# Padded tiles: the start addresses of matmul operands modulo 256 bytes in a two-block transformer kernel

## The chip, the core and the metric

The kernel runs on one core of one Trainium2 chip. The core has five engines with queues of their own: TensorE (PE, with its weight loads listed as PEld), VectorE (DVE), ScalarE (ACT), GpSimd (POOL) and SyncE (SP), and 16 DMA engines that move data between the memory and the on-chip buffer of 128 partitions. A tile lies at one byte address, the same in all its partitions. The metric is the device time of one execution in microseconds (us); the times are medians of some runs.

## What is computed

Two transformer blocks, one after the other, on 256 tokens of width 1024 (batch 1), in float32. Cut to the parts that matter:

```python
def first_block(x, c, ctx, c_ctx, ...):              # two layers
    for layer in range(2):
        ...                                          # adaLN, latent attention over 512 keys, Hyena branch
        x = x + g1 * mix_lat
        x = x + g2 * channel_mixer(rmsnorm(x, norm2_g[layer]) * (1 + sc2) + sh2, layer, ...)
        # layer 0: the context's 256 tokens too, and a dense swiglu of width 2816 on all 512
    return rmsnorm(x, final_g)

def moe_swiglu(h, router, w_gate, w_up, w_down):     # channel mixer of layer 1
    top_val, top_idx = lax.top_k(t @ router, 2)      # 2 of 8 experts for each token
    combine = ...                                    # softmax of the two logits
    for e in range(8):
        out = out + combine[:, e:e + 1] * swiglu(t, w_gate[e], w_up[e], w_down[e])   # width 2816

def second_block(x, c, ...):
    x = sandwich(x, ffn1, ...)     # swiglu, width 2816
    x = sandwich(x, mix, ...)      # chunked attention and a gated linear recurrence
    x = sandwich(x, ffn2, ...)     # swiglu, width 2816
```

## The kernel before

Everything lies transposed, features on the partitions and tokens along the row: 512 columns (256 latent, 256 context) in layer 0, 256 in layer 1's mixer and in the second block. The experts stage works on gathered tokens, up to 128 for each expert.

**Products.** A float32 product is made of three matmuls on operands that are split in a high and a low part (`split`: ACT copies the high part, DVE subtracts it from the source for the low part). `mm3` issues them in the order high·high, high·low, low·high. Each matmul is a weight load of a [128, 128] operand and a stream of 256 or 512 columns of a second one; every matmul of the program has its own load, and the loads of following matmuls overlap the streams (rows PEld and PE).

```python
def mm3(self, out, w, x, start, stop):
    self.mm(out, w[0], x[0], start, False)
    self.mm(out, w[0], x[1], False, False)
    self.mm(out, w[1], x[0], False, stop)
```

**Weights.** A weight tile of 512 KB is loaded into a ring of `raw` tiles (SP's queue), then split into a ring of four pairs `whi` and `wlo`. In the two dense blocks `whi`/`wlo` are the loaded operand and the activations (`h`, `fh`, `mg`, `o`, `rec` in the pools b1 and b3) the streamed one. In the experts stage the roles are the other way: the gathered tokens `xe` (up projections, `acc<-whi,xe`) and the hidden values `hm` (down projection, `y<-whi,hm`) are loaded, and 512 columns of `whi` or `wlo` are streamed (256 in the sixth group of an expert, where the width 2816 leaves a rest). An expert has six groups; each ends its up part with four transposes on PE (`turned`, line 1558), so that a run of equal matmuls is broken there. At the ends of an expert stand `scatter` and, every second one, `gather`.

**Pools.** SBUF is given out in stacks: a pool's tiles lie one behind the other, each rounded up to 32 bytes, and a pool that is opened later starts where the earlier ones end. `cp` and `c1` hold constants; behind them lie `w` (`whi`, `wlo`), `r` (four `raw`), and then either `b1`, `k1` (first block) or `x2` (`xsh`, `xsl`), `r2` (nine more `raw`), `k2` (the experts' tiles, `cmp`, `xe`, `hm0`, `hm1`, `ST`, `ys`), `t2` (`ht`). For the second block `b3` and `k3` are opened behind `x2`, where `r2` to `t2` were. What each tile's size adds moves all that lies behind it.

**Order.** SP and POOL run in the order in which the code stands; PE, DVE and ACT in the order of a scheduler that goes by priorities. Tiles of a ring are reused as their readers finish. The lines that the change touches: `open` (L428, tiles `xsh`, `xsl`), `build` (L651 to L680, constants), `startup` (L725, `tneg`) and `once` inside `moe` (L1643, `cmp`).

Of the kernel before, what the change touches and what calls it, by code (L numbers as in the profile page):

```python
# [8 lines left out]
F32 = mybir.dt.float32  # L9
F32R = mybir.dt.float32r  # L10
# [31 lines left out]
FIRST2 = [("in2", j) for j in range(12, 16)], [(g, 2, i) for i in range(2) for g in "gu"]  # L42
FILTER = 1000
FILTER1 = 3

# [341 lines left out]
class PreNorm:  # L389
# [35 lines left out]
    def open(self):  # L425

        p, sh = self.p, self.parts[0][2]
        hi, lo = (p.xsp.tile([128, 8, 258], F32R, name=n, tag=n, bufs=1) for n in ("xsh", "xsl"))  # L428
        self.xs = [(hi[:, k, :], lo[:, k, :]) for k in range(8)]
        p.split(hi[:, :, 256:], lo[:, :, 256:], sh.unsqueeze(2).to_broadcast([128, 8, 2]))  # L430

# [29 lines left out]
class Prog:  # L461
# [183 lines left out]
    def build(self):  # L645
        nc, tc = self.nc, self.tc
        with ExitStack() as es:
            es.enter_context(tc.manual_schedule(engines={SP, POOL}))
            self.cp = es.enter_context(tc.tile_pool(name="cp", bufs=1))
            self.ps = es.enter_context(tc.tile_pool(name="ps", bufs=1, space=PSUM))  # L650
            self.dp = es.enter_context(tc.tile_pool(name="dp", bufs=1, space=DRAM))  # L651
            cp = self.cp
            self.cv = cp.tile([128, CTOTAL], F32, name="cv")
            self.ident = cp.tile([128, 128], F32, name="ident")
            self.ones = cp.tile([128, 128], F32, name="ones")
            self.epsc = cp.tile([128, 1], F32, name="epsc")
            self.gp = cp.tile([128, 6, 8], F32, name="gp")
            self.sp = cp.tile([128, 8], F32, name="sp")
            self.small = cp.tile([128, 1], F32, name="small")
            self.mod = [cp.tile([128, 2, 48], F32, name=f"mod{l}") for l in range(2)]  # L660
            self.ada = cp.tile([128, 72], F32, name="ada")
            self.gn = cp.tile([128, 16, 8], F32, name="gn")
            self.xt = cp.tile([128, 8, 512], F32, name="xt")
            self.x = [self.xt[:, k, :] for k in range(8)]
            self.xl = [self.xt[:, k, :NT] for k in range(8)]
            self.kspill = [self.dp.tile([128, 2048], F32, name=f"ksp{l}") for l in range(2)]
            self.route = cp.tile([128, 10], F32, name="router")
            self.frn = cp.tile([128, 2, 8], F32, name="frn")

            self.rs = cp.tile([128, 8, 2, 8], F32, name="route")  # L670
            self.cnt = cp.tile([1, 1], I32, name="cnt")
            self.spill = [self.dp.tile([128, 2048], F32, name=f"sp{i}") for i in range(3)]
            nc.vector.memset(self.ones, 1.0)
            nc.vector.memset(self.epsc, EPS)
            self.eps2 = cp.tile([128, 1], F32, name="eps2")
            self.fga = cp.tile([128, 2, 8], F32, name="fga")
            nc.vector.memset(self.eps2, EPS * EPS)
            nc.vector.memset(self.small, 1e-26)
            self.kn, self.early = 512, EARLY[0]
            self.wc, self.turn, self.wbufs, self.wpairs = 1024, [0, 0, 0], [4, 4, 4], []  # L680
            self.hold = ()
            c1 = es.enter_context(tc.tile_pool(name="c1", bufs=1))
            self.rope = c1.tile([128, 2, NT], F32, name="rope")
            self.mcst = c1.tile([128, 128 + 256 + 64 + 64], F32, name="mcst")
            with ExitStack() as s0:
                self.wp, self.rp = (s0.enter_context(tc.tile_pool(name=n, bufs=1)) for n in ("w", "r"))
                with ExitStack() as s1:
                    self.bp = s1.enter_context(tc.tile_pool(name="b1", bufs=13))
                    self.kp = s1.enter_context(tc.tile_pool(name="k1", bufs=1))
                    self.startup()  # L690
                    self.layer0()
                    self.layer1()
                self.xsp = s0.enter_context(tc.tile_pool(name="x2", bufs=1, reuse_waits="tile"))
                self.latter("")

            with tc.If(self.most > 128), ExitStack() as s0:
                self.wp, self.rp, self.xsp = (s0.enter_context(tc.tile_pool(name=n, bufs=1)) for n in ("wg", "rg", "xg"))
                self.latter("g")
# [18 lines left out]
    def startup(self):  # L717
        nc, a = self.nc, self.a
# [3 lines left out]
        hc, hw = (self.b([2048], name=n) for n in ("hc", "hw"))  # L722
        zf = KOFF["zfeat"][0]
        self.dma(hc[:, :256], a["kc"][:, zf:zf + 256])
        self.tneg = self.kp.tile([128, 2], F32, name="tneg")  # L725
        self.dma(self.tneg, a["kc"][:, zf + 256:zf + 258])
        self.dma(hc[:, 512:768], a["hw"][:, :256])
        stages = self.filters(hc, hw)
# [20 lines left out]
        for n, b in enumerate((4, 5, 6, 7, 0, 1, 2, 3)):  # L749
# [20 lines left out]
            for k in range(8):  # L770
                if n not in ADAR:
                    self.mm(acc, cs[:, k, :], w[k // 4][:, k % 4, :], k == 0, k == 7)
                else:
                    hi, lo = w[k // 4][k % 4]
# [4 lines left out]
            for i in range(2):  # L779
                c = 4 * b + 2 * i  # L780
                self.mm(pt[:, c:c + 2], row[:, i * 128:i * 128 + 128], fold[:M], True, True)
            j = 2 * b
            self.tt(m[:, :, j:j + 2], pt[:, 2 * j:2 * j + 4].rearrange("p (b i) -> p i b", i=2),
                    self.col(("bmod", 0), j, 2).unsqueeze(1).to_broadcast([128, 2, 2]), OP.add)
            if n < 4:
                k = j - 8
                self.stt(self.gn[:, 0:2, k:k + 2], m[:, :, j:j + 2], 1.0,
                         self.col(("n1g", 0), k, 2).unsqueeze(1).to_broadcast([128, 2, 2]), OP.add, OP.mult)
                while ready and ready[0] <= k + 1:
                    c = ready.pop(0)  # L790
# [483 lines left out]
    def layer0(self):  # L1274
# [24 lines left out]
        def fill(d):  # L1299
            if d >= FILTER1:  # L1300
                next(filt)
            self.ada_fill(2)
# [114 lines left out]
    def moe(self, tp, general):  # L1417
        nc, kp, tc = self.nc, self.kp, self.tc
# [220 lines left out]
        def once():  # L1639

            for c in range(2):
                self.stt(L[:, c, :], self.lg[c], r[:, c:c + 1], self.route[:, 0:8], OP.mult, OP.add)
            cm = kp.tile([128, 2, 128], F32, name="cmp")  # L1643
            c1, c2 = (cm[:, i, :].rearrange("p (c a b) -> p c a b", c=2, a=8) for i in range(2))
            a = L.unsqueeze(2).to_broadcast([128, 2, 8, 8])
            b = L.unsqueeze(3).to_broadcast([128, 2, 8, 8])
            self.tt(c2, a, b, OP.is_equal)
            self.tt(c2, c2, lt.unsqueeze(1).to_broadcast([128, 2, 8, 8]), OP.mult)
            self.tt(c1, a, b, OP.is_gt)
            self.tt(c1, c1, c2, OP.add)  # L1650
            nc.vector.tensor_reduce(rank, c1, axis=AX.X, op=OP.add)
            masked = self.ts(mask, rank, 1.5, OP.is_lt)
            pp = self.psc(16, "pos")
            self.mm(pp, tri, mask.rearrange("p c e -> p (c e)"), True, False)
            self.mm(pp[:, 8:16], self.ones, mask[:, 0, :], False, True)
            tokens(0, masked)
            nc.vector.tensor_copy(pos, pp.rearrange("p (c e) -> p c e", c=2))

            S0 = onehot(0, 0)
            tokens(1, self.hot)  # L1660
            with tc.issue_after(self.hid):
                self.table(r, AF.Silu)

            pc = self.psc(8, "cnt")
            for c in range(2):
                self.mm(pc, self.ones, mask[:, c, :], c == 0, c == 1)
            nc.vector.reduce_max(rs[:, 7, 1, 0:1], pc, axis=AX.X)
            nc.vector.tensor_copy(self.cnt, rs[0:1, 7, 1, 0:1])
            nc.gpsimd.dma_start(self.spill[0].rearrange("p (a b) -> p a b", a=8), self.xt[:, :, :NT])
            for t, s in zip(ht, self.spill[1:]):  # L1670
                nc.gpsimd.dma_start(s.rearrange("p (a b) -> p a b", a=2), t.bitcast(F32))
            xe = gather(0, S0)
            self.hold = self.got[2:3]
            ready.append(self.whl(*self.last_ahead))
            self.hold = ()
            lows.append(self.lo_ins)
            fetch()
            nxt = {}

            def pair(p):  # L1680
                with tc.issue_after(lows[-8]):
                    nxt["S"] = onehot(0, p)
                nxt["xe"] = gather(p, nxt["S"])
            last = None
            for e in range(NE):
                after = {}
                if e:
                    after[0] = lambda last=last: scatter(*last)
                if e % 2 and e < 7:
                    after[3] = lambda: pair(e // 2 + 1)  # L1690
                elif e % 2 == 0:
                    if e == 0:
                        def late():
                            with tc.issue_after(self.silu), tc.issue_after(lows[-1]):
                                softmax()
                        after[1] = late
                    after[3] = lambda: nxt.update(ST=weights(e // 2, S0))
                y = expert(e, xe, use, used, after)
                last = (e, y, nxt["ST"])
                if e % 2 and e < 7:  # L1700
                    S0, xe = nxt["S"], nxt["xe"]
            return last, lambda: ready
# [276 lines left out]
```

## Time and profile before

| | before |
|---|---|
| median of three runs | 2486.97 us (2485.62 to 2494.7) |
| the profiled execution | 2487.37 us, of which the span is 2484.9 |
| PE busy | 2427.2 us (98%), 13,896 matmuls |
| DVE busy | 1993.1 us (80%) |
| ACT busy | 1499.5 us (60%) |
| POOL busy | 89.2 us (4%) |
| HBM read | 573.87 MB, 233 GB/s over the span |
| experts stage, about | 1045 to 1850 us |
| second block, about | 1850 us to the end |

The profile lists for each instruction when it started and ended. The ends of matmuls are modelled and overlap the next ones, so "mean ns of one" of a matmul is longer than the step from one matmul to the next. How fast PE streams is read from the starts: the timeline gives the start of each group of equal instructions, and the difference of two starts divided by the matmuls between them is the step. Idle time stands with what ended it. The granted clock (PEclk) is a share of full speed.

### The profile page before, as it was taken

The numbers are of one execution on the slowest core, as the hardware profiler recorded it, in microseconds if no ns is written. First come the engines' busy times: TensorE is split into PE (matmuls) and PEld (weight loads), VectorE is DVE, ScalarE is ACT, GpSimd is POOL, SyncE is SP. The second block draws the span as 40 slices with busy tenths as digits, with TensorE's granted clock in tenths as the row PEclk, the third lists the DMA queues.
The fourth block names the chain that finished last, engine by engine and source line by source line (L and its number), as shares of the span: only waits on it lengthen the run. The fifth ranks groups of instructions, "written<-read, shape, count | busy, mean of one in ns | idle before, by whom it ended". The sixth has DMA issues, their size and how long they took to land. (4 is left out here: it accounts for less than half of the span.)

```text
span 2484.9 us, 37467 instructions
## 1 busy us (share of the span) xinstructions
PE 2427.2 (98%) x13896; PEld 2073.1 (83%) x13896; DVE 1993.1 (80%) x3001; ACT 1499.5 (60%) x2214; POOL 89.2 (4%) x170
## 2 busy tenths in 40 slices
PE   8999999999999999999999999999999999999997
PEld 4677887788887898878878888888789999998997
DVE  6787799996878877799888988998986668977555
ACT  6676325422224775687777777777775558667444
POOL 0000010221211000000000000000000000000000
PEclk9999999999999999999999999999999999999999
DMA  7122465787885243799999999999965563444653
GB/s 284 52 87 102 149 223 209 253 290 273 292 290 210 82 142 135 256 364 336 349 341 345 342 345 352 350 333 355 347 232 179 187 212 120 157 168 143 202 182 111
DMA packets 161247, 582.71 MB, mean 235 GB/s; under 512 B 18000, under 2 KB 19536, under 8 KB 159904
## 3 DMA queue, kind: packets, MB, share of 16 engines
q1 hardware_dynamic: 136912, 491.35, 56.0%
q0 software_dynamic: 23600, 88.35, 9.8%
q8 instruction: 111, 1.82, 0.3%
q14 instruction: 80, 0.66, 0.1%
q10 hardware_dynamic: 544, 0.52, 0.1%
HBM read 573.87 MB, written 6.29 MB: 233 GB/s over the span
## 5 line engine op out<-in xcount | busy, mean ns | idle before, releaser
L477 ACT ACTIVATE whi<-raw 128x1024 fp32r<-128x1024 f32 (+1 forms) x902 | 917.9, 1045 | 617.9 <-PE acc L491 385.0
L480 DVE TENSOR_TENSOR wlo<-raw,whi 128x1024 fp32r<-128x1024 f32 (+1 forms) x900 | 1063.6, 1206 | 239.7 <-ACT whi L477 234.0
L491 PE MATMUL acc<-h,whi 128*128 128x256 f32 (+1 forms) x3648 | 840.1, 323 | 9.8 <-ACT h L477 4.6
L491 PEld LDWEIGHTS acc<-h,whi 128*128 128x128 f32 x3648 | 610.0, 189 | 67.8 <-ACT h L477 6.3
L491 PE MATMUL acc<-h,wlo 128*128 128x256 f32 (+1 forms) x1808 | 580.9, 322 | 1.0 <-DVE wlo L480 1.0
L491 PE MATMUL acc<-whi,xe 128*128 128x512 f32 (+1 forms) x1536 | 456.5, 377 | 1.0 <-DVE xe L488 0.7
L491 PEld LDWEIGHTS acc<-h,wlo 128*128 128x128 f32 x1808 | 342.2, 189 | 26.5 <-DVE wlo L480 1.9
L491 PEld LDWEIGHTS acc<-whi,xe 128*128 128x128 f32 x1536 | 280.5, 188 | 54.9 <-DVE xe L488 0.9
L491 PE MATMUL acc<-wlo,xe 128*128 128x512 f32 (+1 forms) x768 | 291.4, 379 | 0.1
L488 DVE SCALAR_TENSOR_TENSOR junk<-wt,rows 128x1024 bf16<-128x1024 f32 x200 | 238.8, 1219 | 4.3 <-DMA wt<-in_w 3.2
L491 PE MATMUL acc<-fh,whi 128*128 128x256 f32 (+1 forms) x1056 | 235.4, 318 | 0.2
L491 PE MATMUL y<-whi,hm 128*128 128x512 f32 x704 | 231.7, 400 | 0.0
L491 PEld LDWEIGHTS acc<-fh,whi 128*128 128x128 f32 x1056 | 174.5, 188 | 14.8 <-DVE fh L480 1.0
L491 PEld LDWEIGHTS acc<-wlo,xe 128*128 128x128 f32 x768 | 144.5, 188 | 30.2 <-DVE wlo L480 3.8
L491 PE MATMUL acc<-fh,wlo 128*128 128x256 f32 (+1 forms) x528 | 167.4, 318 | 0.4 <-DVE wlo L480 0.4
L491 PEld LDWEIGHTS y<-whi,hm 128*128 128x128 f32 x704 | 131.3, 188 | 30.8 <-ACT hm L477 3.1
L491 PE MATMUL y<-wlo,hm 128*128 128x512 f32 x352 | 139.6, 400 | 0.5
L491 PEld LDWEIGHTS acc<-fh,wlo 128*128 128x128 f32 x528 | 99.1, 188 | 7.4 <-DVE wlo L480 0.6
L632 POOL DMA_DIRECT2D wt<-in_w x152 | 81.0, 538 | 344.1 <-DVE junk L488 299.1
L491 PE MATMUL acc<-mg,whi 128*128 128x256 f32 (+1 forms) x384 | 87.7, 321 | 1.0 <-DVE mg L480 1.0
L491 PEld LDWEIGHTS y<-wlo,hm 128*128 128x128 f32 x352 | 66.1, 188 | 18.2 <-DVE wlo L480 3.6
L480 DVE TENSOR_TENSOR a<-a,acc 128x256 f32<-128x256 f32 (+2 forms) x64 | 33.2, 519 | 53.2 <-PE acc L491 52.5
(374 smaller groups left out, 2738.4 us busy)
## 6 DMA issues: line engine op xcount, KB each, us to landing
raw<-in_w SPq DMA_DIRECT2D x890, 512.0 KB, 5.5
wt<-in_w POOLq DMA_DIRECT2D x152, 512.0 KB, 5.9
raw<-in_w SPq DMA_DIRECT2D x24, 384.0 KB, 3.1
xt<-in_x SPq DMA_DIRECT2D x4, 512.0 KB, 9.6
ksp<-hf POOLq DMA_DIRECT2D x2, 1024.0 KB, 6.0
kf<-ksp SPq DMA_DIRECT2D x2, 1024.0 KB, 5.1
sp<-ht POOLq DMA_DIRECT2D x2, 1024.0 KB, 10.7
raw<-in_w SPq DMA_DIRECT2D x8, 256.0 KB, 2.8
```

The source lines that it names most:

```text
L477: return self.nc.scalar.activation(out, in_, func, **kw)
L480: return self.nc.vector.tensor_tensor(out, a, b, op=op)
L488: return self.nc.vector.scalar_tensor_tensor(out, a, s, b, op0=op0, op1=op1, **kw)
L491: return self.nc.tensor.matmul(out, lhsT=lhsT, rhs=rhs, start=start, stop=stop)
L632: self.nc.gpsimd.dma_start(t[:, i, :], self.wsrc(key)[0])
```

## The change

The operations, their order on all five engines and their waits are the same before and after; tiles lie at other addresses.

- Three constant columns of their own (`epsc`, `small`, `eps2`, 32 bytes each with rounding) and `tneg` of the pool `k1` become columns of one tile `few` of 32 bytes. All that lies behind `cp` moves down by 64 bytes, and the tiles of `k1` by 96.
- `cmp`, a tile of the router in `k2`, grows by 40 floats (160 bytes). `S`, `xe`, `hm`, `ST`, `ys` and `ht` lie behind it.
- `xsl` grows by 16 floats (64 bytes). `r2`, and `b3` with `k3` of the second block, lie behind it and so stay where they were.

Where the tiles start, in bytes modulo 256 (worked out by adding the sizes):

| pool, tiles | before | after |
|---|---|---|
| w: `whi`, `wlo` | 64 | 0 |
| r: four `raw` | 64 | 0 |
| b1: all arrays of the first block (`h`, `fh`, `mg`, ...) | 64 | 0 |
| k1: `gq`, `a`, `u`, `ssq`, `nr` | 96 | 0 |
| x2: `xsh`, `xsl` | 64, 128 | 0, 64 |
| r2: nine `raw` | 192 | 192 |
| k2: `xe`, `hm0`, `hm1`, `ST`, `ys` | 96 | 0 |
| k2: `S` | 224 | 128 |
| t2: `ht` | 96 | 0 |
| b3, k3: the second block's arrays and `first` | 192 | 192 |
| cp: `ident`, `ones` | 160 | 160 |
| cp: `xt` | 224 | 192 |

A matmul streams whole chunks of a tile, 128, 256 or 512 columns of 4 bytes apart, so a chunk's residue is that of its tile (but for `xsh` and `xsl`, whose rows have 258 columns).

```diff
+CPAD = 40
+XPAD = 16
...
-        hi, lo = (p.xsp.tile([128, 8, 258], F32R, name=n, tag=n, bufs=1) for n in ("xsh", "xsl"))
+        hi, lo = (p.xsp.tile([128, 2064 + k], F32R, name=n, tag=n, bufs=1)[:, :2064].rearrange("p (a b) -> p a b", a=8)
+                  for n, k in (("xsh", 0), ("xsl", XPAD)))
...
-            self.epsc = cp.tile([128, 1], F32, name="epsc")
+            few = cp.tile([128, 8], F32, name="few")
+            self.epsc, self.eps2, self.small, self.tneg = (few[:, i:j] for i, j in ((0, 1), (1, 2), (2, 3), (3, 5)))
...
-            self.small = cp.tile([128, 1], F32, name="small")
...
-            self.eps2 = cp.tile([128, 1], F32, name="eps2")
...
-        self.tneg = self.kp.tile([128, 2], F32, name="tneg")
...
-            cm = kp.tile([128, 2, 128], F32, name="cmp")
-            c1, c2 = (cm[:, i, :].rearrange("p (c a b) -> p c a b", c=2, a=8) for i in range(2))
+            cm = kp.tile([128, 256 + CPAD], F32, name="cmp")
+            c1, c2 = (cm[:, 128 * i:128 * i + 128].rearrange("p (c a b) -> p c a b", c=2, a=8) for i in range(2))
```

## Rows read from the trace of the kernel before

**Rows 1.** Busy time by stretch: PE, PEld, DVE, ACT, POOL, then PEclk, DMA share, GB/s.

```profile
1045.00:1850.00 805.00, 801.63 (x3824) 652.98 (x3822) 718.31 (x758) 602.45 (x686) 0.00 (x0) 1.00 0.95 344
1850.00:2485.00 635.00, 609.30 (x4921) 597.05 (x4919) 432.00 (x702) 379.60 (x663) 0.00 (x0) 0.98 0.49 162
1100.00:1150.00 50.00, 50.00 (x251) 41.57 (x251) 45.16 (x44) 39.94 (x44) 0.00 (x0) 1.00 0.97 363
```

**Rows 2.** Waits, 1100 to 1840: waiter, releaser, us in total, times, longest.

```profile
ACT whi L477 <- DMA raw<-in_w: 4.2, 10, 0.7
PEld acc L491 <- DVE wlo L480: 3.8, 11, 0.5
```

**Rows 3.** Timeline of PE, layer 0's feed-forward: start, us, instruction, count.

```profile
600.04 0.39 PE L491 MATMUL acc<-h,wlo 128*128 128x512 f32 x1
...
619.76 0.39 PE L491 MATMUL acc<-h,wlo 128*128 128x512 f32 x1
```

**Rows 4.** Timeline of PE, experts stage, 512 columns.

```profile
1377.98 0.40 PE L491 MATMUL acc<-wlo,xe 128*128 128x512 f32 x1
...
1387.77 0.40 PE L491 MATMUL acc<-wlo,xe 128*128 128x512 f32 x1
```

**Rows 5.** Instructions by form, 1045 to 1850: count, busy us, mean ns.

```profile
L491 PE MATMUL acc<-whi,xe 128*128 128x512 f32 x1280 | 409.5, 396 | 1.0 <-DVE xe L488 0.7 <-ACT whi L477 0.2
L491 PE MATMUL acc<-wlo,xe 128*128 128x512 f32 x640 | 255.4, 399 | 0.1
L491 PE MATMUL y<-whi,hm 128*128 128x512 f32 x704 | 231.7, 400 | 0.0
L491 PE MATMUL y<-wlo,hm 128*128 128x512 f32 x352 | 139.6, 400 | 0.5
L491 PE MATMUL acc<-whi,xe 128*128 128x256 f32 x256 | 47.0, 282 | 0.0
L1558 PE MATMUL tp<-ident,xt 128*128 128x128 f32 x176 | 27.0, 272 | 0.0
```

**Rows 6.** Busy time of PE in stretches of layer 0: us, count, PEclk, DMA share, GB/s.

```profile
500.00:520.00 20.00, 20.00 (x90) 1.00 0.58 203
520.00:540.00 20.00, 20.00 (x90) 1.00 0.95 354
```

**Rows 7.** Timeline of PE behind a broken run in layer 0.

```profile
274.94 0.39 PE L491 MATMUL acc<-oh,wlo 128*128 128x512 f32 x1
276.09 0.39 PE L491 MATMUL acc<-h,whi 128*128 128x512 f32 x1
```

**Rows 8.** Timeline of PE, 256 columns: layer 1, then the experts' sixth group.

```profile
900.05 0.28 PE L491 MATMUL acc<-h,wlo 128*128 128x256 f32 x1
901.49 0.28 PE L491 MATMUL acc<-h,wlo 128*128 128x256 f32 x1
1330.91 0.28 PE L491 MATMUL acc<-wlo,xe 128*128 128x256 f32 x1
1336.24 0.28 PE L491 MATMUL acc<-wlo,xe 128*128 128x256 f32 x1
```

**Rows 9.** Timeline of PE, 256 columns, second block: first and last feed-forward.

```profile
1949.83 0.28 PE L491 MATMUL acc<-h,wlo 128*128 128x256 f32 x1
1969.77 0.28 PE L491 MATMUL acc<-h,wlo 128*128 128x256 f32 x1
2419.80 0.28 PE L491 MATMUL acc<-h,wlo 128*128 128x256 f32 x1
2421.24 0.28 PE L491 MATMUL acc<-h,wlo 128*128 128x256 f32 x1
```

**Rows 10.** PE with tile whi, then with tile wlo, 1850 to 2485: us, count.

```profile
1850.00:2485.00 635.00, 546.41 (x3008) 0.98 0.49 162
1850.00:2485.00 635.00, 423.62 (x1504) 0.98 0.49 162
```

**Rows 11.** Layer 0's attention scores, tile gq: count, min/median/max ns, starts, forms.

```profile
L491 PE MATMUL sc<-kt,gq x96: 278/387/503, 102.1 to 218.5; 96*128 96x512 f32 x48, 96*128 96x256 f32 x48
```

## Prediction

> **What bounds the kernel now.** I read the busy times by stretch first, then the waits of the long stretch, then the starts of matmuls in the timeline. In the experts stage PE is busy 801.6 of 805 us at a granted clock of 1.00 [rows 1], and what waits there waits for PE, or briefly: ScalarE waits for a weight tile's DMA 4.2 us in ten places, and a weight load for the low parts 3.8 us [rows 2]. In the second block PE is busy 609.3 of 635 us [rows 1]. So TensorE's own pace sets the time, and since the operations, their order and their waits stay as they are, the change can work only through that pace: the step from one matmul to the next in an unbroken run.
>
> The reader should divide differences of starts. In layer 0's feed-forward 87 matmuls of 512 columns lie between the two low-part rows of [rows 3]: 19.72 us / 87 = 226.7 ns. In the experts stage 42 matmuls of the same shape lie between those of [rows 4]: 9.79 us / 42 = 233.1 ns. Both have the full clock, both run without a gap. In layer 0 the loaded tile (whi, 64) and the streamed one (h, 64) start at equal residues modulo 256; in the experts stage the loaded one is at 96 (xe, hm) and the streamed one at 64 (whi, wlo). I write a case as streamed minus loaded: 0 in layer 0, 224 (32 short of equal) in the experts. Traffic is not what differs: in layer 0 two neighbouring stretches of 20 us hold 90 matmuls each, one with 203 GB/s of DMA beside it and one with 354 [rows 6].
>
> At 256 columns the picture is another: layer 1 (difference 0) takes 1.44 us / 12 = 120.0 ns, the experts' sixth group (224) 5.33 us / 45 = 118.4 [rows 8], the second block (128) 19.94 us / 168 = 118.7 in its first feed-forward and 1.44 us / 12 = 120.0 near its end [rows 9]. So one difference, 128, shows two paces, and equality isn't the faster case there.
>
> **The change part by part.** After it the experts' pairs lie at difference 0, the first block's stay at 0, and the second block's go from 128 to 192.
>
> Experts, 512 columns: 1280 + 640 + 704 + 352 = 2976 matmuls [rows 5], each from 233.1 to 226.7 ns: 2976 x 6.4 ns = 19.0 us less. I take layer 0's step because it is the row with the same shape and the same difference.
>
> Broken runs: the pace has to be found again after a break. In layer 0 the five matmuls behind one took 276.09 - 274.94 = 1.15 us, 230 ns each [rows 7], 3.3 ns over the settled pace. The transposes break the experts' runs 176 / 4 = 44 times [rows 5], scatters and gathers some 16 more: 60 x 5 x 3.3 ns = 1.0 us of the gain is lost.
>
> Experts, 256 columns: 256 of whi [rows 5], and half as many of wlo since mm3 streams the high part twice: 384. From 118.4 to layer 1's 120.0 ns: 0.6 us more.
>
> Second block: 3008 + 1504 = 4512 matmuls on whi and wlo [rows 10], and no row shows a difference of 192. Bounds: a matmul of 256 columns can hardly step faster than half of 226.7, or 113.3 ns, so at best 4512 x 5.4 = 24.4 us less; at worst it pays the same 6.4 ns that 512 columns pay for a bad offset, 28.9 us more. I take nothing, by the nearest rows: 192 lies between 128 and 224, and these show 118.7 and 118.4. The spread of the rows, 118.4 to 120.0, is 1.3 ns about the value taken, or 5.9 us either way.
>
> Small pieces: layer 0's scores with the tile gq (96 to 0) have 48 matmuls of 512 columns [rows 11], at most 48 x 6.4 ns = 0.3 us less, in an attention stage of short runs where I count nothing; if the new address were as bad as the old one is against the settled pace, as much more. The two runs on xsh and xsl, 192 matmuls of 258 columns, could move by 1.2 us either way by the same 6.4 ns. The merged constants add no instruction and no wait.
>
> What must keep up: a triple of matmuls falls from 0.699 to 0.680 us, and the work that feeds it is hidden now. DVE is busy 718.3 of 805 us and would be so of some 787, 91%; DMA would need 344 x 805 / 787 = 352 GB/s where one stretch of 50 us shows 363 [rows 1]. Both fit, so I cost the cover at nothing; if it gave way, part of the gain would turn into waits of ScalarE for weight tiles, and then of weight loads for the split.
>
> Sum: 2487.4 (the profiled execution's own time, 0.4 above the median) - 19.0 + 1.0 + 0.6 = 2470.0, and 2469.6 against the median of 2487.0: **2470**.
>
> **The rivals.** *Addresses are not the cause.* Rows 3 and 4 also differ in which tile is streamed and in what ACT and DVE do beside. Then nothing moves: 2487. For it: only one difference other than 0 is shown at 512 columns. Against it: the steps in the experts stage are as even as those of layer 0, the 14 triples of [rows 4] at 0.69 to 0.70 us, though the work beside them comes and goes. The Trainium skill speaks for this rival: "SBUF — State Buffer", section "Who interferes with whom", gives TensorE two independent read ports, one for the stream and one for the weight load, and says that it never waits on anyone; by that rule the place of two operands could not matter and the time stays at 2487. The two steps of [rows 3, 4] don't fit it, since shape and clock are the same.
>
> *The second block gains as well.* At 192 its runs might settle at a faster pace than any row shows. Half of the bound, 12 us, gives 2458, all of it 2446. For it: difference 128 already shows that two paces are possible [rows 9]. Against: none of four rows at 256 columns is under 118.4.
>
> *The other side.* At 192 the second block's streams and loads hinder each other as they do at 512 columns in the experts stage. At 6.4 ns more for each of 4512 matmuls it is 28.9 us against a gain of 17.4: 2499. It decides from 17.4 us / 4512 = 3.9 ns on, a step of 122.6 ns. Against it: at 256 columns the difference of 224 costs nothing [rows 8]. A small loss, to 120.0 ns everywhere, gives 2476 and belongs to the forecast's own range.
>
> *The feed gives way.* PE asks for weights 2% faster; if DMA or the split held the stage at half of the gain, the time would be 2478. For it: the ten waits for DMA [rows 2]. Against: the 363 GB/s.
>
> **How the numbers follow.** Forecast, experts at 226.7 and the second block within 1.3 ns of now: 0.67, own range 2464 to 2476. No effect of addresses, 2487: 0.09. Second block gains, 2446 to 2462: 0.13. Slower, 2482 to 2499: 0.05. Feed gives way, about 2478: 0.06. The range of 8 in 10 goes from 2455 to 2482: the forecast, the feed, and half of the second block's gain. What a measurement of this kernel can tell from no change is about 0.5%, 12.4 us, or a time under 2474.5. Of the forecast 0.06 lies above that, with the second block near 120.0: faster 0.61 + 0.13 = 0.74, same 0.06 + 0.09 + 0.06 = 0.21, slower 0.05.
>
> **What would show it.** Right: in the timeline of the changed kernel runs of the experts stage step by 226 to 227 ns (triples of 0.68 us), the stage ends some 17 us earlier, layer 0 keeps 226.7, the waits for DMA stay under 10 us, and the second block keeps steps of 118 to 120. Wrong: experts' triples still at 0.70 us (addresses are not the cause); triples at 0.68 with the stage not shorter, and waits of ScalarE on DMA or of weight loads on the low parts in its place (the feed); or the second block's step outside 117.4 to 120.0, which moves the time by 4.5 us for each ns.

## The result, and the profile after

The changed kernel takes 2459.0 us, the kernel before 2490.8, both medians of four runs; the ratio, 0.9871 with a 95% interval of 0.9849 to 0.9894, leaves out one run of the changed kernel that took 3987.8 us at a granted clock of 0.555, so that its other three, 2456.2 to 2460.6 us, stand for it. It is faster by 1.3%. The prediction had the sign and a range that holds the time, but not the make-up of the gain, as its stages show.

Stages can be cut at three starts in the timeline of PE: the first matmul of layer 0 (at 48.6 us in both), the first matmul on the experts' tokens, and the last one on `y`. Here are the last two, first of before, then of after (start, us, instruction, count).

```profile
1047.68 0.50 PE L491 MATMUL acc<-whi,xe 128*128 128x512 f32 x1 [0.73 <-DVE xe L488]
...
1845.64 0.40 PE L491 MATMUL y<-whi,hm 128*128 128x512 f32 x1
```

```profile
1049.64 0.50 PE L495 MATMUL acc<-whi,xe 128*128 128x512 f32 x1
...
1836.12 0.39 PE L495 MATMUL y<-whi,hm 128*128 128x512 f32 x1
```

With the ends of the spans (2484.9 and 2458.1) that makes:

| us | first block | experts | second block |
|---|---|---|---|
| before | 999.1 | 798.0 | 639.2 |
| after | 1001.1 | 786.5 | 622.0 |
| difference | +2.0 | -11.5 | -17.2 |

The +2.0 comes with the clock. PE's matmuls stand in the same order in both, and after falls 2.4 us behind between 206 and 273 us, where its granted clock went down to 0.5 (1.2 GHz, the lower of the two levels) for 6.8 us from 233 us on; over 226 to 250 us PEclk is 0.86 there and 1.00 in before. Just ahead of the fall, from 226 to 233.1 us, PE was busy 5.67 us in after, and 5.76 in before, where the clock stayed. In the runs below that have the first block's differences as in after this stage takes 1000.1 to 1006.4 us. So the experts brought two thirds of what was forecast for them, and the second block, for which nothing was forecast, brought more than the experts.

The page and the busy times by stretch answer to [rows 1]. The stretches of after are the experts stage, the second block, a run of 69 matmuls in the experts stage and a run of 575 in the second block; columns as there.

```profile
span 2458.1 us, 37467 instructions
...
PE 2400.1 (98%) x13896; PEld 2054.5 (84%) x13896; DVE 1991.8 (81%) x3001; ACT 1500.0 (61%) x2214; POOL 89.6 (4%) x170
```

```profile
1047.00:1840.00 793.00, 789.97 (x3821) 650.82 (x3819) 717.00 (x756) 602.17 (x685) 0.00 (x0) 1.00 0.95 350
1840.00:2458.00 618.00, 591.33 (x4922) 578.60 (x4922) 431.83 (x702) 380.32 (x664) 0.00 (x0) 0.98 0.51 167
1213.59:1229.04 15.45, 15.45 (x69) 12.77 (x68) 14.87 (x16) 12.40 (x14) 0.00 (x0) 1.00 0.91 313
1897.38:1962.44 65.06, 65.06 (x575) 65.06 (x575) 33.25 (x37) 33.36 (x49) 0.00 (x0) 1.00 0.60 195
```

The first row reads like that of before: PE is busy 99.6% of the experts stage at the full clock, DVE's work is the same 717 us in a shorter time, and DMA moves 350 GB/s. A stretch that is cut at the first and the last start of an unbroken run holds one step less than matmuls (a matmul or two that still run at its edge may add to the count). So the third row is 68 steps of 512 columns, 15.45 us / 68 = 227.2 ns, and the fourth 574 steps of 256 columns, 65.06 / 574 = 113.3 ns: the value that the prediction held for the floor.

The waits of after between 1100 and 1840 answer to [rows 2].

```profile
ACT whi L481 <- DMA raw<-in_w: 6.3, 13, 1.8
PEld acc L495 <- DVE wlo L484: 6.1, 23, 0.5
```

Both have grown, from 4.2 and 3.8 us, and are still small.

Layer 0 is as in [rows 3]: between these two rows lie 87 matmuls, 19.72 us, 226.7 ns each.

```profile
600.27 0.39 PE L495 MATMUL acc<-h,wlo 128*128 128x512 f32 x1
...
619.99 0.39 PE L495 MATMUL acc<-h,wlo 128*128 128x512 f32 x1
```

### The profile page after: what moved, and what is told of

The parts are those of the page before. It is cut to its first block, busy times and chain, and to the rows that moved or that the text cites. A ratio compares the mean times of both kernels' runs of the same rounds, so it can differ in the third digit from the quotient of the medians.

```text
span 2458.1 us, 37467 instructions
## 1 busy us (share of the span) xinstructions
PE 2400.1 (98%) x13896; PEld 2054.5 (84%) x13896; DVE 1991.8 (81%) x3001; ACT 1500.0 (61%) x2214; POOL 89.6 (4%) x170
## 5 line engine op out<-in xcount | busy, mean ns | idle before, releaser
L495 PE MATMUL acc<-h,whi 128*128 128x256 f32 (+1 forms) x3648 | 829.4, 321 | 9.6 <-ACT h L481 4.6
L495 PE MATMUL acc<-whi,xe 128*128 128x512 f32 (+1 forms) x1536 | 451.0, 373 | 0.3 <-ACT whi L481 0.3
L495 PE MATMUL acc<-fh,whi 128*128 128x256 f32 (+1 forms) x1056 | 230.3, 315 | 0.7 <-DVE fh L484 0.6
L481 ACT ACTIVATE hm<-tp 128x512 fp32r<-128x512 f32 (+1 forms) x48 | 26.9, 561 | 75.0 <-PE tp L1561 74.9
```

The lines of the kernel that those rows point to most:

```text
L481: return self.nc.scalar.activation(out, in_, func, **kw)
L495: return self.nc.tensor.matmul(out, lhsT=lhsT, rhs=rhs, start=start, stop=stop)
```

## The experiments

The theory after the result: what sets PE's step is the residue of the streamed operand minus that of the loaded one, modulo 256 bytes; 512 columns are fastest at a difference of 0, 256 columns at 192. Each experiment gives one stage another difference by the size of a pad, with the order of the work as it was. Its two knobs are CPAD (it moves the experts' tiles) and XPAD (it moves the second block's arrays). In all kernels with a pad alone PE, DVE, ACT and POOL run the same instructions in the same order as in after. Times with a ratio and its interval are medians of five to seven runs; the other kernels ran once, beside one run of before. Single runs of before lie between 2484.4 and 2495.3 us, so that for a kernel that ran once the stages and steps of its trace count, and not its whole time.

### Each half alone

`cpad_only`, the experts at 0 and the second block at 128 as before:

```diff
-CPAD = 40
-XPAD = 16
+CPAD = 56
+XPAD = 0
```

> XPAD 0 and CPAD 56 in the changed kernel: the first block's and the experts' pairs stay at difference 0 as in the changed kernel, the second block's arrays lie at 128, so its difference is 128 as before the change. Theory (the step is set by where the streamed and the loaded operand start modulo 256, each stage for itself): experts settle at 226.7 ns as in the changed kernel, stage about 11 us shorter than before; the second block's feed-forwards step by 118.7 to 120 ns, its span about 634 us; whole time 10 to 12 us under before, about 2476. Rival (the second block's gain comes from the weights at address 0, or from the merged constants): second block at 113.3 ns, whole time about 2459.

`xpad_only`, the second block at 192 and the experts at 224 as before:

```diff
-CPAD = 40
+CPAD = 48
```

> CPAD 48: only the experts' tiles are moved, to 32 modulo 256, so that the experts have difference 224 as before the change (and a start that isn't a multiple of 64), while the second block keeps 192. Theory: experts at 233 ns again, stage 798 us as before, second block at 113.3 and 117.6 ns, 617 us; whole time about 17 us under before, 2470. Rival (the experts' gain is one of absolute places or of traffic): experts stay at 227 to 229 ns and the time at 2459.

Measured: `cpad_only` 2477.9 us, 0.9961 of before (0.9942 to 0.9980), experts 786.0 and second block 635.4 us; `xpad_only` 2476.1 us, 0.9942 (0.9921 to 0.9962), experts 797.8 and second block 623.3 us. The two gains are separate. By the stages they add up, 12.0 us in the experts of the one and 15.9 us in the second block of the other beside 28.7 in both stages of after; the whole times give 9.7 and 14.4 beside 32.1 us, each with an interval of about 5 us either way. The second block of `xpad_only` is 6 us longer than was expected. The same two runs of matmuls that stand above for after, here the experts' 68 steps in before and in `xpad_only`, then the second block's 574 in `cpad_only`:

```profile
1214.36:1230.22 15.86, 15.86 (x70) 12.78 (x68) 15.09 (x16) 12.40 (x14) 0.00 (x0) 1.00 0.90 309
```

```profile
1218.31:1234.17 15.86, 15.86 (x70) 12.77 (x68) 15.08 (x16) 12.39 (x14) 0.00 (x0) 1.00 0.91 312
```

```profile
1899.47:1967.58 68.11, 68.11 (x576) 68.11 (x575) 33.34 (x37) 33.47 (x49) 0.00 (x0) 1.00 0.56 186
```

15.86 / 68 = 233.2 ns and 68.11 / 574 = 118.7 ns: each stage falls back to its old step, with DMA (312 against 313 GB/s), DVE and ACT beside it as in after.

### The experts at other differences

`exp_d192` gives the experts the difference at which the second block gained, `exp_d128` and `exp_d64` the two between:

```diff
-CPAD = 40
+CPAD = 56      # exp_d192;  72 in exp_d128, 88 in exp_d64
```

> CPAD 56: the experts' loaded tiles go from 0 to 64, so that the streamed operand lies 192 beyond the loaded one, as in the second block; all else as in the changed kernel. Theory (192 is the fastest place for any width, and 64-byte starts are all that 512 columns need besides): 512 columns settle at 220 ns (233.1 less two of the 6.67 ns by which the steps so far differ), the experts stage 10 to 20 us shorter than in the changed kernel, time 2440 to 2450. Rival (512 columns are best at equality): 227 to 233 ns, time 2459 to 2471. Second rival (pace is better but the feed takes over): 220 ns in runs, more waits for DMA and low parts, time about 2459.

> The experts' tiles xe and hm start 128 bytes from the weight tiles modulo 256 instead of at the same residue; the second block stays at a difference of 192. Theory (512-column runs have one fast case, equality, at 226.7 ns, and one slow one, 233 ns, everywhere else): experts' steps of 233, the experts stage about 798 us, the run about 2471. Rival (the step grows with the distance from equality, up to half the period): steps over 234 and a stage over 800. Second rival (128 is as good as 0 for 512 columns, the pattern having a period of 128): steps of 227, stage 786, the run 2459.

> The experts' tiles xe and hm at 192 against the weight tiles at 0, or a difference of 64; the second block stays at 192. Theory (equality alone is fast for 512 columns): steps of 233 ns, a stage of about 798 us, the run about 2471. Rival (a sign: differences on one side of equality, as 192 and 224, are slow and those on the other are not): steps of 227, stage 786, the run 2459. At 256 columns 64 is a new difference: no theory gives a value, 113 to 120 ns.

Measured: `exp_d192` 2475.3 us, 0.9935 (0.9913 to 0.9956), experts 797.4; `exp_d128` 2473.9 beside 2494.0, experts 796.6; `exp_d64` 2467.7 beside 2494.0, experts 788.9. The run of 68 steps in `exp_d192`, then in `exp_d64`:

```profile
1221.39:1237.26 15.87, 15.87 (x69) 12.79 (x68) 15.04 (x16) 12.42 (x14) 0.00 (x0) 1.00 0.90 302
```

```profile
1218.72:1234.29 15.57, 15.57 (x69) 12.77 (x68) 14.99 (x16) 12.40 (x14) 0.00 (x0) 1.00 0.93 316
```

233.4 ns at 192 and 229.0 at 64; at 128 the same run takes 232.5. So 192 isn't good for every width, and equality is the best of five differences for 512 columns. But "one fast case, and one slow one everywhere else" falls too: 64 is a third case, nearer to the fast one.

### The first block at 192

`b1_d192` puts a tile of 192 bytes ahead of the first block's arrays:

```diff
-XPAD = 16
+XPAD = 32
+                self.rp.tile([128, 48], F32, name="bpad", tag="bpad", bufs=1)
```

> A tile of 192 bytes ahead of the first block's pools (and XPAD 32): the first block's arrays lie at 192 and its weights at 0, so layer 0 (512 columns) and layer 1 (256 columns) have difference 192 instead of 0; experts at 0 and second block at 192 as in the changed kernel. Theory (192 is the fastest place for any width): layer 0's feed-forward steps by 220 ns instead of 226.7, layer 1 by 113.3 to 117.6 instead of 120; some 3700 matmuls of 512 columns and 1200 of 256 give 20 to 30 us, time 2430 to 2440. Rival (512 columns are best at equality): layer 0 at 226.7 or 233, layer 1 alone gains 3 to 7 us, time 2450 to 2480.

Measured: 2477.5 us, 0.9954 (0.9936 to 0.9971), so some 20 us over after by the two ratios, and the first block 1015.4 us, 14.3 over that of after. Layer 0's longest unbroken run, 1583 steps of 512 columns, in after and then in `b1_d192`:

```profile
444.30:803.14 358.84, 358.84 (x1584) 297.21 (x1583) 293.32 (x467) 111.43 (x147) 67.52 (x126) 1.00 0.76 276
```

```profile
452.91:822.28 369.37, 369.37 (x1585) 297.60 (x1583) 295.33 (x467) 110.68 (x147) 67.25 (x126) 1.00 0.75 268
```

226.7 against 233.3 ns: layer 0, where the roles are the other way (weight tiles are loaded, activations streamed), has the same two steps as the experts. It is the difference, and not the tile or what runs beside it. Layer 1, with 256 columns, went the other way in the same run, from 119.7 to 116.3 ns in the mean of its steps. The run shows one thing more: both pads together move the experts' loaded tiles by 256 bytes against their weight tiles, and the experts stay at 786.6 us and a mean step of 228.7 ns. So a shift of 256 bytes changes nothing, while one of 128 does, as `exp_d128` shows.

### The second block at other differences

`blk2_d0` and `blk2_d64`; the experts stay at 0:

```diff
-CPAD = 40
-XPAD = 16
+CPAD = 24      # blk2_d0;  8 in blk2_d64
+XPAD = 32      # blk2_d0;  48 in blk2_d64
```

> The second block's arrays at the residue of its weights, a difference of 0 instead of 192; the experts stay at 0. Theory (256 columns are slow at equality, as in layer 1): second-block steps of 119 to 120 ns, that stage 637 to 642 us, the run 2475 to 2480. Rival (the second block gained because of another effect of the move than its difference of 192, such as the arrays' distance to each other): steps of 113 to 118 stay and the run takes about 2460.

> The second block's arrays at a difference of 64 from its weights; experts at 0. Nearest known: 256 columns at 0 and 128 take 119 to 120 ns and at 192 113 to 118. Theory (one fast case, 192, as 512 columns have one at 0): steps of 118 to 120 ns, the second block 635 to 641 us, the run 2474 to 2480. Rival (the two odd multiples of 64 are alike, a period of 128): steps of 113 to 118, the block 622 us, the run 2459.

Measured: `blk2_d0` 2480.1 us beside 2494.0, second block 641.9; `blk2_d64` 2477.2 beside 2493.2, second block 631.0. The run of 574 steps in `blk2_d0`:

```profile
1898.21:1967.08 68.87, 68.87 (x575) 68.87 (x575) 33.38 (x37) 33.51 (x49) 0.00 (x0) 1.00 0.57 184
```

and in `blk2_d64`, with its fellow of the same 574 steps in the second feed-forward:

```profile
1905.87:1973.48 67.61, 67.61 (x576) 67.61 (x576) 33.35 (x37) 33.47 (x49) 0.00 (x0) 1.00 0.58 187
2324.28:2389.33 65.05, 65.05 (x575) 65.05 (x575) 35.06 (x40) 32.30 (x48) 0.00 (x0) 1.00 0.63 194
```

At equality 120.0 ns, as in layer 1; the theory holds. At 64 one run goes at 117.8 ns and the like one at 113.3: there are two paces at one difference, and a run keeps the one that it has got into. Neither expectation for `blk2_d64` is right: the block lies between them. The slower of the two paces is found at 192 as well. `exp_d128` has the second block of after, address for address, and there the first of these runs took:

```profile
1906.57:1974.18 67.61, 67.61 (x576) 67.61 (x575) 33.34 (x37) 33.48 (x49) 0.00 (x0) 1.00 0.59 187
```

117.8 ns where after has 113.3. That makes its second block 626.7 us instead of 622.0, and it happened by itself: nothing was changed there. Over all kernels with 192 the second block took 619.5 to 626.7 us.

### The same differences at other addresses

`all32` moves everything behind the constants by 32 bytes, so that no operand starts at a multiple of 64:

```diff
-            few = cp.tile([128, 8], F32, name="few")
+            few = cp.tile([128, 16], F32, name="few")
```

> Everything behind the small constants moves by 32 bytes, so that no operand of the experts or the second block starts at a multiple of 64, while all differences stay as in the changed kernel. Theory (only the difference of the two addresses counts): experts' steps 227 to 229 ns, second block 113 to 118 ns, the run 2456 to 2463. Rival (what counts is that operands start at a multiple of 64 bytes): the experts' steps go back to 233 and the second block's to 119, and the run to about 2487.

Measured: 2461.8 us beside 2494.0, experts 786.3, second block 621.8. The two runs again:

```profile
1215.05:1230.49 15.44, 15.44 (x70) 12.76 (x68) 14.89 (x16) 12.41 (x14) 0.00 (x0) 1.00 0.90 300
```

```profile
1898.56:1963.62 65.06, 65.06 (x576) 65.06 (x575) 33.25 (x37) 33.36 (x49) 0.00 (x0) 1.00 0.62 195
```

227.1 and 113.3 ns: where both operands move by 32 bytes, the steps stay. Layer 0 kept its 226.7 ns as well when both its operands moved by 64 bytes, from before to after. So the difference counts, and not where the two lie, as far as these two moves show.

### Why the experts gained less than forecast

The pair `nobreak_224` and `nobreak_0` is without the transposes that break the experts' runs:

```diff
-                    tp = self.ptp(n)
-                    for i in range(n // 128):
-                        nc.tensor.transpose(...)
-                    self.split(t[0], t[1], tp)
+                    self.split(*(x.rearrange("p (a b) -> p a b", a=c) for x in t), a)
```

> The experts stage without the transposes of the hidden values (the split reads the activations' tile directly; that part of the computation is left out), with the experts' operands at a difference of 224 as before the change; second block at 192. It is the partner of the next run: only the difference between the two counts. The stage should be some 25 to 40 us shorter than with transposes; its 512-column steps 233 ns.

> The same without the transposes, with the experts' operands at equal residues. Theory (the breaks by the transposes eat the part of the experts' gain that is missing, since 8 or 9 matmuls behind each run at 231 ns before they settle): the experts stage is 15 to 19 us shorter than in the run at 224, nearer to 2976 x 6.4 = 19.0 us than the 11.5 us with transposes. Rival (the waits for weight loads and transfers eat it, and stay): the difference stays at 11 to 13 us, with more waits in the run at 0.

Measured: experts 777.1 us at 224 and 769.9 at 0, 7.2 us apart, less than the 11.5 with the transposes. The theory fell, and the rival's 11 to 13 us weren't met either; `nobreak_224` is 20.7 us shorter than `xpad_only`, where 25 to 40 were expected. By the steps alone the gain is 13.7 us (2862 steps, from 233.1 to 228.3 ns), so waits took back about half of it. The waits of weight loads between 1060 and 1800 us, in `nobreak_224` and then in `nobreak_0`:

```profile
PEld acc L495 <- DVE wlo L484: 8.9, 34, 0.4
```

```profile
PEld acc L495 <- DVE wlo L484: 15.4, 43, 0.5
```

So the rival has the right sign: without the breaks a faster PE catches up with DVE's subtraction, and waits 6.5 us more for it. In after, with the breaks, these waits were 6.1 us: the breaks cost PE time, but they also give the feed time to keep up.

`half_nb_0` tried to take that feed away:

```diff
+                elif self.half and n == 1024:
+                    self.act(hi, raw)
+                    self.lo_ins = self.tt(lo[:, :512], raw[:, :512], hi[:, :512].bitcast(F32), OP.subtract).ins
```

> The experts stage without the transposes of the hidden values and with half of the subtractions for the weights' low parts (512 of each tile's 1024 columns; the matmuls on low parts read those twice; both parts of the computation are left out there), operands at equal residues. Without the transposes alone the stage is 769.9 us at equal residues and 777.1 at a difference of 224, only 7.2 us apart, and waits of weight loads for low parts are 15.4 against 8.9 us. Theory (at the faster pace VectorE's subtraction holds the stage there, and the transposes had been its slack): with VectorE relieved these waits fall under 5 us, more of the runs settle at 226.7 ns and the stage is 758 to 764 us, 13 to 19 us under 777.1. Rival (what keeps the runs from settling is neither VectorE nor the transposes): waits may fall, but the stage stays at 766 to 770 us and the mean step of 512 columns at 228 ns or more.

Measured: the stage takes 787.9 us, longer than with the whole subtraction. It became another kernel: the scheduler set the order anew, so that 209 of ScalarE's 2214 instructions and 719 of PE's matmuls stand at other places than in `nobreak_0`. Its waits in the same stretch:

```profile
ACT xt L481 <- PE acc L495: 116.7, 42, 3.3
...
PEld acc L495 <- ACT whi L481: 18.2, 38, 0.7
PEld acc L495 <- DVE wlo L484: 16.8, 35, 0.5
```

ScalarE now stands 116.7 us (59.2 in `nobreak_0`) before an expert's SiLU, with the splits of weight tiles queued behind it, and PE has 45 steps of over 600 ns where `nobreak_0` has one. This run doesn't tell the two theories apart. What it does show: between the stalls 2369 of 2860 steps run at 226 or 227 ns (1949 of 2862 in `nobreak_0`, 1748 of 2855 in after), and in the middle of a settled run the pace is lost without a stall not once (41 and 48 times).

## The differences in one table

Means over the steps between neighbouring starts of one stage, stalls left out (steps up to 15% over the median), in ns; the length of the stage in us.

| difference | 512 columns, experts | stage | 256 columns, second block | stage |
|---|---|---|---|---|
| 0 | 228.6 (`all32` too) | 786.5 | 119.9 | 641.9 |
| 64 | 230.0 | 788.9 | 116.8 | 631.0 |
| 128 | 232.6 | 796.6 | 118.9 (before) | 639.2 (635.4 in `cpad_only`) |
| 192 | 233.3 | 797.4 | 114.5 | 622.0 |
| 224 | 233.1 (before) | 798.0 | 119.0 (experts' 256) | |

The experts' own runs of 256 columns agree with the fourth column, though the roles are the other way there: 119.7 ns at 0, 116.7 at 64, 118.7 at 128, 114.7 at 192.

## Why the prediction was right, and where it was not

**What bounds the kernel.** Right: PE's own pace set both stages. With the work and its order unchanged, a shorter step turned into a shorter stage, within 1.0 us of the sum of the steps in the experts (12.5 and 11.5) and within 1.5 in the second block (18.7 and 17.2).

**Experts, 2976 x 6.4 = 19.0 us.** Right in mechanism and in the settled step: the longest runs of after step by 227.2 ns where before has 233.2. By the starts, the steps up to 245 ns went from 2861 of 233.1 ns to 2855 of 228.7, 12.5 us. The rest, 1.0 us the other way, is in the steps over 245 ns (121, 115 before; 74 of each stand beside a matmul of another form, the others are stalls), the 256-column runs and the transposes.

**Broken runs, 1.0 us.** This is the term that was mis-sized: it is 5.8 us. In after 1107 of the 2855 steps aren't at 226 or 227 ns, and they average 5.2 ns more. The prediction had 300 of them (60 breaks of 5) at 3.3 ns. Here is a run behind four transposes, in the timeline of after (each row is the third matmul of a triple):

```profile
1374.23 0.40 PE L495 MATMUL acc<-wlo,xe 128*128 128x512 f32 x1
1374.92 0.40 PE L495 MATMUL acc<-wlo,xe 128*128 128x512 f32 x1
1375.62 0.39 PE L495 MATMUL acc<-wlo,xe 128*128 128x512 f32 x1
1376.30 0.39 PE L495 MATMUL acc<-wlo,xe 128*128 128x512 f32 x1
1376.98 0.40 PE L495 MATMUL acc<-wlo,xe 128*128 128x512 f32 x1
1377.68 0.39 PE L495 MATMUL acc<-wlo,xe 128*128 128x512 f32 x1
1378.36 0.39 PE L495 MATMUL acc<-wlo,xe 128*128 128x512 f32 x1
```

Two triples at 0.69 and 0.70 us, two at the settled 0.68, then one at 0.70 again. Behind such a break it mostly takes eight or nine matmuls, not five, to settle. And there are more breaks: the 1107 steps lie in 230 stretches, of which 37 begin behind the transposes and 72 behind the matmuls of `gather` and `scatter` and their tables. The prediction counted 44 and 16 (the transposes stand in 48 places, since the sixth group of an expert has only two of them). These 109 stretches cost 3.3 us. Of the others 8 begin behind 256 columns, 26 behind a stall and 39 are only the last step of a run, 1.2 us together; 48 begin in the middle of a settled run, like the triple of 0.70 us above, and cost 1.4 us. In `nobreak_0`, without the transposes, 913 such steps still cost 4.7 us. [rows 7] showed five matmuls of layer 0, in a stage where runs of 1583 steps stay settled: no measure for a stage where DVE follows closely.

What goes with a loss in the middle of a run can be seen in the weight loads, here those of the last triples:

```profile
1376.30 0.41 PEld L495 LDWEIGHTS acc<-whi,xe 128*128 128x128 f32 x2
1376.82 0.19 PEld L495 LDWEIGHTS acc<-wlo,xe 128*128 128x128 f32 x1
1376.98 0.42 PEld L495 LDWEIGHTS acc<-whi,xe 128*128 128x128 f32 x2
1377.45 0.19 PEld L495 LDWEIGHTS acc<-wlo,xe 128*128 128x128 f32 x1
```

The load at 1376.82 begins 0.11 us after the end of the one before it, that at 1377.45 0.05 us. PE doesn't stall for it, and the rows of waits don't count it, since they begin at 0.15 us. In 46 of the 48 places a weight load began more than 60 ns after the end of the one before it (39 ns are usual), 45 times because it waited for DVE's `wlo`. Of the 63 steps of settled runs with such a load 46 lost the pace, of the 1591 without one 2. `half_nb_0`, with half of these subtractions, has no such load in its settled runs and no such loss; `nobreak_0` has 34, and 27 of its 41 losses are there. By this a subtraction that comes a little late costs a run its settled pace. No run moved that alone, though, and why the pace is lost for several matmuls stays open.

**Experts, 256 columns, 0.6 us more.** Their mean went from 119.0 to 119.7 ns: 384 x 0.7 = 0.3 us.

**Second block, 0.** This is the step that failed: 17.2 us came where none were forecast, with a mean step of 114.5 ns. By the prediction's own sign, a step outside 117.4 to 120.0, its forecast was wrong here, and 2459 lies outside the forecast's own 2464 to 2476; the wider 2455 to 2482 holds it because half of this gain was let in. It was taken as nothing because 192 lies between 128 and 224, which both showed 118 to 119 ns. The pace isn't smooth in the difference: 128, 192 and 224 give 118.9, 114.5 and 119.0. The bound, half of 226.7 ns, was right to the decimal, and long runs reach it; the prediction gave no reason for it but the half, so that is luck in part. The mean is 114.5 and not 113.3 mainly because the 1311 steps outside the runs of 168 matmuls or more take 116.3 ns in the mean; one long run of after, 277 matmuls, went at 117.8 and adds 0.3 ns. The rival that gave 2446 to 2462 had the mechanism and the size, and a chance of 0.13 that the rows did not support: no row of before shows 256 columns at 192, and the row at 128 that shows two paces spoke for more doubt than 1.3 ns.

**Small pieces.** The scores with `gq` take 23.8 us in both, and the matmuls of 258 columns went from 43.3 to 42.6: inside their bounds.

**The feed.** Cost at nothing, and nearly right in size: waits for DMA 6.3 us and for low parts 6.1, together 4.4 more than before, with stalls of PE up by 0.5 us. But it is nearer than the prediction thought, as `nobreak_0` and the losses in settled runs show.

**The other rivals.** That addresses aren't the cause is refuted by the pads: 6.6 ns appear and vanish in layer 0 and in the experts with one pad. The Trainium skill ("SBUF — State Buffer", section "Who interferes with whom") gives TensorE independent ports for its two operands, from which this rival took that their places can't matter. In these runs they do, 226.7 against 233.3 ns with shape, clock and order equal, and the measurement decides. The loss at 192 has its place in the experts (`exp_d192`, +10.9 us), not in the second block.

That the forecast of 2470 came within 11 us of 2459 is in part luck: the experts' missing 5.9 us and the second block's 17.2 have opposite signs.

## What to carry to other kernels

Where a trace shows TensorE streaming without a gap, divide long differences of starts by their matmuls and compare stages of the same width: if the steps differ at the same clock, look at where the streamed and the loaded tile start modulo 256 bytes. Try the residues (the two pads of this change cost 64 and 160 bytes), since neither the best one nor its sign carries over from one width to another, and values between measured differences can't be interpolated. A step that is settled in a long run is not what a stage of short runs gets, so take the step of a broken stage from a broken stage.

## What the runs showed of the hardware

- At a granted clock of 1.00 (2.4 GHz, the upper of its two levels) the fast steps, 226.7 and 113.3 ns, are 544 and 272 cycles, 17/16 of 512 and 256 columns; the slow step of 512 columns, 233.3 ns, is 560.
- At 256 columns and a difference of 64 or 192 two paces, 113.3 and 117.8 ns, are both stable over 574 steps, and which one a run gets can change from one execution's trace to another's at the same addresses (65.06 and 67.61 us for the same run in after and `exp_d128`). At 128 the last feed-forward's run, which went at 120.0 in before [rows 9], took 118.7 in `cpad_only`, at the same difference. In all kernels at 64 and 192 each of the second block's runs of 168 matmuls or more goes at 113.3 to 113.5 or at 117.8 ns in its mean, and none between.
- DMA's traffic beside the second block's run of 574 steps was 184 to 195 GB/s, in inverse proportion to the run's length: the same bytes in 65.05 to 68.87 us, so it does not explain the step.
- Why the difference of the two starts matters, and what chooses between the two paces, no run here shows.
